# Splitting the weights of a two-layer decoder with casting and adding DMA transfers from GpSimd instead of a VectorE subtraction

## The chip, the cores and the metric

The kernel runs on one core of one Trainium2 chip. The metric is the device time of one execution in microseconds; before the change three runs gave a median of 1575.38 us (1574.05 to 1576.89).

A core has five engines with their own instruction streams: PE (TensorE, matrix products; PEld is its weight loads), ACT (ScalarE), DVE (VectorE), POOL (GpSimd) and SP (SyncE, which only issues transfers here). Sixteen DMA engines move data between memory (HBM) and the on-chip SBUF. Each engine works its stream in order and waits on semaphores where it needs another's result.

## The reference

A decoder trunk on 512 tokens of width 1024, with two layers. Each layer is a mixer, a cross-attention into 256 memory tokens, and a gated MLP, all on normalised inputs and added to the running x.

```python
for l in range(DEPTH):                       # DEPTH = 2
    h = rmsnorm(x, norm_mix[l])
    if l % 2 == 0:                           # conv branch + differential attention
        x = x + even_mixer(h, even_w_in[e], ..., even_w_out[e], lam_init)
    else:                                    # stick-breaking attention, 16 heads
        x = x + odd_mixer(h, odd_w_qkv[o], odd_w_out[o])
    x = x + mem_attention(rmsnorm(x, norm_xattn[l]), rmsnorm(mem, norm_mem[l]),
                          x_w_q[l], x_w_kv[l], x_q_gain[l], x_k_gain[l], x_w_out[l])
    x = x + conv_ffn(rmsnorm(x, norm_ffn[l]), ffn_w_up[l], ffn_conv[l], ffn_w_down[l])
return x

def conv_ffn(h, w_up, w_conv, w_down):       # w_up 1024 x 5632, w_down 2816 x 1024
    u = causal_dwconv(h @ w_up, w_conv)
    gate, val = jnp.split(u, 2, axis=-1)
    return (jax.nn.silu(gate) * val) @ w_down
```

All inputs and outputs are float32. What matters for the change are the products `h @ w`: every weight matrix is used once per execution, against all 512 tokens (or all 256 memory tokens for `x_w_kv`).

## The kernel before

**Two parts per operand.** Every float32 operand is carried as hi + lo, both of the type float32r: hi is the value rounded to float32r, lo is what is left. A product of two such operands takes three matmuls, hi x hi, hi x lo and lo x hi (`lin_stream`). For activations and for weights alike, ACT writes hi (a cast) and DVE writes lo = source - hi (`split`, and for weights `prep`).

**The weight stream.** `weight_groups` lists all weights in the order of use, as groups of four column chunks of 128 (or eight, or two) by up to eight chunks of 128 rows. They lie in memory as 260 slots of 128 x 1024 float32 (512 KB), most groups being four slots. `loads` (L571) issues one SP transfer per slot into a `raw` buffer; `prep` (L589) casts it into a `hi` buffer on ACT (L388) and subtracts it into a `lo` buffer on DVE (L403), then frees the raw buffer. The pools hold 3 raw, 5 hi and 5 lo buffers, handed out in turn. The first group (`V`) is loaded in halves of 256 KB, between the chunks of x.

**The matmuls.** `lin` starts one `lin_stream` for each column chunk (or token block) of a group; each accumulates over all row chunks into one of three PSUM accumulators (`acc`) and then spawns the work that takes the result out. In a gated-MLP group of four slots A, B, C, D each slot holds two row chunks of four columns, so a column takes six matmuls of each slot, and the group 96 matmuls of 512 columns. A slot's hi and lo buffers are free when its last column has used them. All four slots are read by every column, so the buffers come free only while the last column runs. The groups of the memory's keys and values (`KV`) have only two token blocks and take 48 matmuls for four slots.

**What sets the order.** The program is written as streams that yield operations. `Issue` keeps a modelled clock per engine, gives each operation a modelled duration, and puts the operations in one static order per engine: of those that can start first, the one with the smallest priority number. An allocation (`AL`) waits until a pool has a free buffer. So the order of a queue such as SP's or POOL's is fixed when the program is built, and at run time each instruction waits, in that order, for the semaphores of what it needs. POOL's stream holds the adds of the norms' squares (`nacc`), small powers for the norms (`s`, `k`), masks and clears (L452, L457); it issues no transfer.

**Names in the profile.** `acc<-hs,hi` and `acc<-hs,lo` are matmuls of activation chunks with weight parts, `acc<-h,...`, `acc<-hi,hs` and the like the same with other activation tiles or the operands exchanged. `raw<-wts` is a weight load, `hi<-raw` ACT's cast, `lo<-raw,hi` DVE's subtraction. L439 is `mm`, L448 `dma`.

Of the kernel before, what the change touches and what calls it, by code (L numbers as in the profile page):

```python
# [14 lines left out]
ALU = mybir.AluOpType  # L15
# [16 lines left out]
def weight_groups():  # L32
    """(name, source, layer, k-chunks, column starts of the 128-wide column chunks)"""
# [95 lines left out]
class T:  # L129
    """a tile and the times of its last accesses"""  # L130
# [55 lines left out]
class Op:  # L186
    __slots__ = ("eng", "dur", "reads", "writes", "fn")

    def __init__(self, eng, dur, reads, writes, fn):
        self.eng, self.dur, self.fn = eng, dur, fn  # L190
        self.reads = [x for x in reads if isinstance(x, V)]
        self.writes = [x for x in writes if isinstance(x, V)]
# [17 lines left out]
class Issue:  # L210
# [24 lines left out]
    def issue(self, op, start):  # L235
        ins = None
        prev = self.last.get(op.eng)
        if prev is None:
            ins = op.fn()
        else:  # L240
            with self.tc.issue_after(prev):
                ins = op.fn()
        self.last[op.eng] = ins.ins
        if op.eng == "SP":
            self.free_at["SP"] = start + 0.5
            b = max(start + 1.2, self.dma_at)
            self.dma_at = b + op.dur
            end = self.dma_at + 1.0
        else:
            end = start + op.dur  # L250
            self.free_at[op.eng] = end
        self.issued(op, start, end, ins.ins)
        for x in op.reads:
            assert x.t.known, "an operation reads a tile that none before it writes"
            for p in x.parts():
                x.t.r[p] = max(x.t.r[p], end + LAT[op.eng])
        for x in op.writes:
            x.t.known = True
            for p in x.parts():
                x.t.w[p] = (end, op.eng)  # L260
# [80 lines left out]
def trunk(ctx: ExitStack, tc: tile.TileContext, xT: bass.AP, memT: bass.AP, wts: bass.AP, par: bass.AP, outT: bass.AP):  # L341
# [11 lines left out]
    pRAW = pool("raw", 3)  # L353
    pHI = pool("hi", 5)
# [94 lines left out]

    def memset(out, val):  # L450
        out = vw(out)
        return Op("POOL", 0.05 + out.n() * 0.0007, [], [out], lambda: nc.gpsimd.memset(out.ap, val))  # L452
# [15 lines left out]
    def stack_q(qs, ps):  # L468
        """qs[s]: rows of part s: hi; the other 64 rows: lo (s = 0, 1: rows 0-63, 64-127 of ps)"""
        for s, (a, b) in enumerate(HALVES):  # L470
            yield act(qs[s][a], ps[a])
            yield tt(qs[s][b], ps[a], qs[s][a].f32(), ALU.subtract)

    def stack_k(kd, kl, ps, scale=None):
        """kd[s]: part s of ps, hi, in both halves of the rows; kl: lo"""
        for s, (a, b) in enumerate(HALVES):
            sc = 1.0 if scale is None else scale[a]
            yield act(kd[s][a], ps[a], scale=sc)
            if scale is None:
# [43 lines left out]
    def warm():  # L523
        """keeps the tensor engine busy until the first operands are there, for its clock"""
# [6 lines left out]
    def setup2():  # L531
# [16 lines left out]
        # dist[p, c] = p + 384 - c: query row p of the block whose slice ends at column 512  # L548
# [18 lines left out]
    raws, prepped = {}, {}  # L567
# [3 lines left out]
    def loads():  # L571
        for gi in range(len(GROUPS)):
            for d in extra.get(gi, ()):
                yield from d()
            for s in range(NSLOT[gi]):
# [9 lines left out]
                else:  # L585
                    yield dma(raw.v(), src, SLOT)
                raws[gi, s] = raw

    def prep():  # L589
        for gi in range(len(GROUPS)):  # L590
            for s in range(NSLOT[gi]):
                hi, lo = yield [AL(pHI, F32R, (P, SLOT), parts=2), AL(pLO, F32R, (P, SLOT), parts=2)]
                if gi == 0:
                    for j in range(2):
                        js = slice(j * 512, j * 512 + 512)
                        yield Until(lambda: (gi, s, j) in raws)
                        raw = raws[gi, s, j]
                        yield act(hi[:, js].p(j), raw[:, js].p(j))
                        yield tt(lo[:, js].p(j), raw[:, js].p(j), hi[:, js].p(j).f32(), ALU.subtract)
                        prepped[gi, s, j] = (hi, lo)  # L600
                else:
                    yield Until(lambda: (gi, s) in raws)
                    raw = raws[gi, s]
                    yield act(hi, raw)
                    yield tt(lo, raw, hi.v().f32(), ALU.subtract)
                    prepped[gi, s, 0] = prepped[gi, s, 1] = (hi, lo)
                free(raw)
# [49 lines left out]
    def lin_done(*names):  # L657
        """all matmuls of these groups have been issued"""
# [19 lines left out]
    def rpow(out, src, n, scale):  # L678
        """out = (src * scale + eps) ** -0.5"""
# [57 lines left out]
    # x chunks: F[name, k] is the tile once its last update has been issued  # L737
# [10 lines left out]
    # ================= layer 0 mixer =================  # L748
# [10 lines left out]
    def qk_even(name, N):  # L759
        # [s][128, head, token]  # L760
# [50 lines left out]
    def put_pt(th, tl, src, i, done=None):  # L811
        """transpose the (i+1) key chunks of query block i and store them at key chunk c, query block i"""
# [99 lines left out]
    def conv3(src, wname, base, step, t):  # L912
        """causal width-3 depthwise convolution along the tokens"""
# [37 lines left out]
    class Lazy(dict):  # L951
        """activation chunks that appear as they are produced"""
# [64 lines left out]
    def head_norm(ps, rc):  # L1017
        """[128 tokens, 2 heads x 256]: normalised, and its transpose [features, (head, dc, token)]"""
# [175 lines left out]
    # ================= gated MLP =================  # L1194
# [83 lines left out]
        # 1 where the key is not strictly before the query (same slicing as dist)  # L1278
# [32 lines left out]
    def stick_head(pr, j):  # L1311
# [10 lines left out]
        for c in range(NB):  # L1322
# [4 lines left out]
            # rows 0-63: hi parts' product and hi x lo; rows 64-127: lo x hi  # L1327
# [23 lines left out]
    def stick(xin, xout):  # L1351
# [4 lines left out]
        def proj(a):  # L1356
# [18 lines left out]
            # [128 keys, key chunk, head, hi | lo, 64]  # L1375
# [103 lines left out]
    spawn(loads(), 3.0)  # L1479
    spawn(prep(), 3.0)  # L1480
# [44 lines left out]
```

## Time and profile before

| | |
|---|---|
| three runs, median (lowest to highest) | 1575.38 us (1574.05 to 1576.89) |
| profiled execution, span from first to last instruction | 1574.8 us |
| PE busy in it | 1550.8 us |
| DVE, ACT, POOL busy | 1048.2, 750.0, 175.7 us |
| granted TensorE clock, mean | 0.997 |
| read from memory in all | 142.92 MB |

The profile gives the span of the profiled execution and no other time of it; the median of the runs is 0.6 us longer. How to read it: the busy share of an engine is an average over stages. The chain of work that ended last is followed back from the end and names, for each stretch of time, the engine and line that set it; idle time of an engine off that chain costs nothing. In the groups of instructions a row reads: line, engine, operation, out<-in, shapes, count | busy us, mean ns of one | idle time of the engine before them and what ended it. In the views of stretches (windows) a row holds the stretch, its length, each engine's busy time with its count of instructions, the granted clock, the share of the 16 DMA engines that is busy, and GB/s.

### The profile page before, as it was taken

How to read it: one execution, taken by the hardware profiler on the slowest of the kernel's cores; microseconds unless marked ns; L12 is line 12 of the kernel's file. 1: busy time of each engine (PE TensorE's matmuls, PEld its weight loads, DVE VectorE, ACT ScalarE, POOL GpSimd, SP SyncE). 2: the span in 40 equal slices, each digit the busy share in tenths (PEclk: the TensorE clock that was granted, in tenths of full speed). 3: DMA queues.
4: the chain of work that ended last, by engine and by line, in shares of the span. 5: the costliest groups of instructions: out<-in, count | busy, mean ns of one | idle time of the engine just before them, and what ended most of it. 6: DMA issues, size and time to landing. Idle time of an engine off the chain costs nothing.

```text
span 1574.8 us, 19182 instructions
## 1 busy us (share of the span) xinstructions
PE 1550.8 (98%) x7242; PEld 1264.2 (80%) x7242; DVE 1048.2 (67%) x1594; ACT 750.0 (48%) x1298; POOL 175.7 (11%) x218
## 2 busy tenths in 40 slices
PE   8999999999999999999999999999999999999999
PEld 6776788788788888888888778787887888888887
DVE  6687756565777457555688887876566765477443
ACT  6566445553534234323577777664544443244221
POOL 4211220200200000000321121202002000000000
PEclk9999999999999999999999999999999999999999
DMA  6212436321233332233221112252113223332232
GB/s 205 70 54 67 127 104 194 110 68 54 64 97 107 107 96 83 89 107 107 81 81 54 48 61 81 80 175 94 54 54 106 88 76 106 107 107 93 76 99 80
DMA packets 42428, 146.26 MB, mean 93 GB/s; under 512 B 4832, under 2 KB 4832, under 8 KB 42336
## 3 DMA queue, kind: packets, MB, share of 16 engines
q1 hardware_dynamic: 42336, 145.04, 29.5%
q8 instruction: 57, 0.93, 0.2%
q14 instruction: 35, 0.29, 0.1%
HBM read 142.92 MB, written 2.10 MB: 92 GB/s over the span
## 4 chain that ended last, share of the span: by engine, by line
PE 88%; DVE 6%; POOL 2%; issue 2%; ACT 2%; DMA 0%; SPq 0%; POOLq 0%; DVEq 0%; ACTq 0%
PE acc L439 77%; PE sc L439 5%; PE pv L439 3%; PE tr L443 3%; POOL nacc L403 2%; DVE hs L409 1%; DVE lo L403 1%; DVE x L403 1%; DMA x<-xT 0%; PE tr L439 0%; ACT hs L391 0%; DVE g L1300 0%; DVE g L403 0%; ACT hi L388 0%; DVE h L403 0%
## 5 line engine op out<-in xcount | busy, mean ns | idle before, releaser
L439 PE MATMUL acc<-hs,hi 128*128 128x512 f32 x1952 | 615.4, 394 | 0.2
L439 PEld LDWEIGHTS acc<-hs,hi 128*128 128x128 f32 x1952 | 365.6, 189 | 78.9 <-issue 3.2
L388 ACT CAST hi<-raw 128x1024 fp32r<-128x1024 f32 (+1 forms) x264 | 271.9, 1035 | 244.4 <-PE acc L439 171.7
L439 PE MATMUL acc<-hs,lo 128*128 128x512 f32 x976 | 383.4, 393 | 4.4 <-DVE lo L403 4.3
L403 DVE TENSOR_TENSOR lo<-raw,hi 128x1024 fp32r<-128x1024 f32 (+1 forms) x264 | 321.9, 1231 | 60.9 <-ACT hi L388 57.9
L439 PE MATMUL acc<-hi,hs 128*128 128x512 f32 (+1 forms) x960 | 280.8, 370 | 0.9 <-ACT hs L391 0.7
L439 PEld LDWEIGHTS acc<-hs,lo 128*128 128x128 f32 x976 | 184.0, 189 | 44.2 <-DVE lo L403 5.7
L439 PE MATMUL acc<-h,hi 128*128 128x512 f32 x704 | 216.2, 389 | 0.0
L439 PEld LDWEIGHTS acc<-hi,hs 128*128 128x128 f32 x960 | 173.1, 190 | 33.6 <-issue 3.1
L439 PE MATMUL acc<-lo,hs 128*128 128x512 f32 (+1 forms) x480 | 176.0, 368 | 5.6 <-DVE lo L403 5.6
L409 DVE SCALAR_TENSOR_TENSOR g<-c,pp,g 128x511 f32<-128x511 f32 (+1 forms) x176 | 132.1, 750 | 56.7 <-ACT g L391 53.6
L403 DVE TENSOR_TENSOR x<-x,acc 128x512 f32<-128x512 f32 x104 | 70.8, 683 | 145.0 <-PE acc L439 144.9
L439 PEld LDWEIGHTS acc<-h,hi 128*128 128x128 f32 x704 | 132.1, 188 | 27.5
L391 ACT ACTIVATE g<-c,pp 128x512 f32<-128x512 f32 x88 | 63.7, 723 | 154.4 <-DVE c L403 154.4
L439 PE MATMUL acc<-h,lo 128*128 128x512 f32 x352 | 136.4, 389 | 0.0
L403 POOL TENSOR_TENSOR nacc<-nacc,sq 128x512 f32<-128x512 f32 x36 | 56.8, 1578 | 524.5 <-ACT sq L391 475.0
L403 DVE TENSOR_TENSOR c<-acc,rrow 128x512 f32<-128x512 f32 x92 | 63.5, 691 | 70.8 <-PE acc L439 63.9
L439 PEld LDWEIGHTS acc<-lo,hs 128*128 128x128 f32 x480 | 90.8, 189 | 22.0 <-DVE lo L403 7.3
L439 PE MATMUL acc<-y,hi 128*128 128x512 f32 x256 | 81.5, 394 | 0.6 <-ACT y L388 0.6
L439 PEld LDWEIGHTS acc<-h,lo 128*128 128x128 f32 x352 | 66.1, 188 | 13.7
L403 DVE TENSOR_TENSOR g<-g,g 128x512 f32<-128x512 f32 (+2 forms) x112 | 64.7, 578 | 7.8 <-ACT g L388 1.4
L391 ACT ACTIVATE g<-sc,rq 128x128 f32<-128x128 f32 (+3 forms) x128 | 60.9, 530 | 8.8 <-PE sc L439 6.5
(157 smaller groups left out, 1624.7 us busy)
## 6 DMA issues: line engine op xcount, KB each, us to landing
raw<-wts SPq DMA_DIRECT2D x256, 512.0 KB, 4.1
x<-xT SPq DMA_DIRECT2D x16, 256.0 KB, 4.8
raw<-wts SPq DMA_DIRECT2D x8, 256.0 KB, 5.9
raw<-memT SPq DMA_DIRECT2D x4, 512.0 KB, 4.2
outT<-x SPq DMA_DIRECT2D x8, 256.0 KB, 2.0
pp<-par SPq DMA_DIRECT2D x1, 303.5 KB, 5.4
pp<-par SPq DMA_DIRECT2D x1, 4.0 KB, 1.7
```

The lines of the kernel that those rows point to most:

```text
L388: return nc.scalar.copy(out=out.ap, in_=in_.ap)
L391: return nc.scalar.activation(out=out.ap, in_=in_.ap, func=func, scale=_raw(scale), **kw)
L403: lambda: _ve(eng).tensor_tensor(out=out.ap, in0=in0.ap, in1=in1.ap, op=op))
L409: lambda: nc.vector.scalar_tensor_tensor(out=out.ap, in0=in0.ap, scalar=_raw(scalar), in1=in1.ap, op0=op0, op1=op1))
L439: lambda: nc.tensor.matmul(out.ap, lhsT.ap, rhs.ap, start=start, stop=stop))
L443: return Op("PE", 0.109, [in_, ident_v], [out], lambda: nc.tensor.transpose(out.ap, in_.ap, ident_v.ap))
```

## The change

From the second group on, a slot is no longer loaded raw by SP, cast by ACT and subtracted by DVE. Instead POOL issues a casting transfer from memory into the hi buffer (`prep_hi`), ACT writes lo = -hi, and POOL issues a second transfer of the same weights that adds them to the lo buffer (`accum_op=ALU.add`), which makes lo = w - hi. The raw pool goes from 3 to 2 buffers, the hi pool from 5 to 6. The first group keeps the old path. `Op` and `Issue` get a modelled duration for POOL's transfers (1.1 us of POOL's time in the model); removed comments and blank lines are left out here.

```diff
-    __slots__ = ("eng", "dur", "reads", "writes", "fn")
+    __slots__ = ("eng", "dur", "reads", "writes", "fn", "land")
...
+        elif op.land is not None:
+            self.free_at[op.eng] = start + op.dur
+            b = max(start + op.dur + 1.0, self.dma_at)
+            self.dma_at = b + op.land
             end = self.dma_at + 1.0
...
-    pRAW = pool("raw", 3)
-    pHI = pool("hi", 5)
+    pRAW = pool("raw", 2)
+    pHI = pool("hi", 6)
     pLO = pool("lo", 5)
...
+    def pool_dma(out, in_, n, **kw):
+
+        out = vw(out)
+        return Op("POOL", 1.1, [out] if kw else [], [out], lambda: nc.gpsimd.dma_start(out=out.ap, in_=in_, **kw),
+                  land=n * P * 4 / 358.0e3)
...
-            for s in range(NSLOT[gi]):
+            for s in range(NSLOT[gi] if gi == 0 else 0):
...
-                else:
-                    yield dma(raw.v(), src, SLOT)
                 raws[gi, s] = raw
+
+    def prep_hi():
+
+        for gi in range(1, len(GROUPS)):
+            for s in range(NSLOT[gi]):
+                if gi == 1 and s == 0:
+                    yield Until(lambda: (0, NSLOT[0] - 1) in raws)
+                hi = yield AL(pHI, F32R, (P, SLOT), parts=2)
+                yield pool_dma(hi, wts[FIRST[gi] + s], SLOT)
+                his[gi, s] = hi
 
     def prep():
         for gi in range(len(GROUPS)):
             for s in range(NSLOT[gi]):
+                if gi:
+                    yield Until(lambda: (gi, s) in his)
+                    hi = his[gi, s]
+                    lo = yield AL(pLO, F32R, (P, SLOT), parts=2)
+                    yield act(lo, hi.v().f32(), scale=-1.0)
+                    yield pool_dma(lo, wts[FIRST[gi] + s], SLOT, accum_op=ALU.add)
+                    prepped[gi, s, 0] = prepped[gi, s, 1] = (hi, lo)
+                    continue
...
-                else:
-                    yield Until(lambda: (gi, s) in raws)
-                    raw = raws[gi, s]
-                    yield act(hi, raw)
-                    yield tt(lo, raw, hi.v().f32(), ALU.subtract)
-                    prepped[gi, s, 0] = prepped[gi, s, 1] = (hi, lo)
                 free(raw)
...
     spawn(loads(), 3.0)
+    spawn(prep_hi(), 2.95)
     spawn(prep(), 3.0)
```

How the instructions are placed, at two points inside the first gated MLP.

The weight transfers for one group. Before, they stand on SP, one per slot, each waiting for the DVE subtraction that frees a raw buffer:

```order
L448 DMA raw_4678<-wts 128x1024 [waits DMAHW1_49,DVE_49]
L448 DMA raw_4690<-wts 128x1024 [waits DMAHW2_49,DVE_49]
L448 DMA raw_4702<-wts 128x1024 [waits DMAHW3_49,DVE_49]
L448 DMA raw_4724<-wts 128x1024 [waits DMAHW4_49,DVE_49]
L448 DMA raw_4806<-wts 128x1024 [waits DMAHW5_49,DVE_49]
```

Now they stand on POOL, eight per group. With A, B, C, D for a group's slots, the first two rows are hi of C and D, the next two hi of A and B of the following group, then lo of B, C, D and of the following A. A hi row waits for PE (the buffer of six allocations earlier), a lo row for ACT's lo = -hi; DMASW are the semaphores of POOL's earlier transfers:

```order
L458 DMA hi_4842<-wts 128x1024 [waits DMASW3_49,PE_49]
L458 DMA hi_4855<-wts 128x1024 [waits DMASW4_49,PE_49]
L458 DMA hi_4864<-wts 128x1024 [waits DMASW5_49,PE_49]
L458 DMA hi_4874<-wts 128x1024 [waits DMASW6_49,PE_49]
L458 DMA lo_4843<-wts 128x1024 [waits DMASW7_49,Activation_49]
L458 DMA lo_4887<-wts 128x1024 [waits DMASW0_49,Activation_49]
L458 DMA lo_4899<-wts 128x1024 [waits DMASW1_49,Activation_49]
L458 DMA lo_4910<-wts 128x1024 [waits DMASW2_49,Activation_49]
```

SP issued the loads of a group as raw buffers came free; POOL now issues all four hi transfers ahead of the first lo transfer, and both kinds stand in one queue.

The matmuls of the same stage on PE. Before, a column (one accumulator) goes through all four slots in one piece; hi_4827, hi_4940 are the group's slots A and B:

```order
L439 MATMUL acc_4899<-hs_3655,hi_4827 128x512
L439 MATMUL acc_4899<-hs_3656,hi_4827 128x512
L439 MATMUL acc_4899<-hs_3655,lo_4828 128x512
L439 MATMUL acc_4899<-hs_3657,hi_4827 128x512
L439 MATMUL acc_4899<-hs_3658,hi_4827 128x512
L439 MATMUL acc_4899<-hs_3657,lo_4828 128x512
L439 MATMUL acc_4899<-hs_3659,hi_4940 128x512
L439 MATMUL acc_4899<-hs_3660,hi_4940 128x512
L439 MATMUL acc_4899<-hs_3659,lo_4941 128x512
```

Now three columns (acc_4809, acc_4838, acc_4880) first take slot A and two hi products of slot B, eight matmuls each, and only then does the first column go on with lo_4843 (B), hi_4842 and lo_4887 (C), hi_4855 and lo_4899 (D). These are the 23rd to the 34th matmul of the group:

```order
L444 MATMUL acc_4880<-hs_3594,hi_4727 128x512
L444 MATMUL acc_4880<-hs_3595,hi_4727 128x512
L444 MATMUL acc_4809<-hs_3594,lo_4843 128x512
L444 MATMUL acc_4809<-hs_3596,hi_4727 128x512
L444 MATMUL acc_4809<-hs_3597,hi_4727 128x512
L444 MATMUL acc_4809<-hs_3596,lo_4843 128x512
L444 MATMUL acc_4809<-hs_3598,hi_4842 128x512
L444 MATMUL acc_4809<-hs_3599,hi_4842 128x512
L444 MATMUL acc_4838<-hs_3594,lo_4843 128x512
L444 MATMUL acc_4809<-hs_3598,lo_4887 128x512
L444 MATMUL acc_4809<-hs_3641,hi_4842 128x512
L444 MATMUL acc_4809<-hs_3642,hi_4842 128x512
```

The first use of the lo tiles of B, C and D has moved behind the start of three columns: lo of B is read first by the 25th matmul of the group, lo of C by the 32nd, lo of D by the 39th. The last column still takes the four slots one after the other, six matmuls each.

More of the change, by code (lines that the diff above doesn't have):

```diff
@@ L186, with __init__ @@
 class Op:
-    __slots__ = ("eng", "dur", "reads", "writes", "fn")
-    def __init__(self, eng, dur, reads, writes, fn):
-        self.eng, self.dur, self.fn = eng, dur, fn
+    __slots__ = ("eng", "dur", "reads", "writes", "fn", "land")
+    def __init__(self, eng, dur, reads, writes, fn, land=None):
+        self.eng, self.dur, self.fn, self.land = eng, dur, fn, land
         self.reads = [x for x in reads if isinstance(x, V)]
@@ L247, in issue @@
             self.dma_at = b + op.dur
+            end = self.dma_at + 1.0
+        elif op.land is not None:
+            self.free_at[op.eng] = start + op.dur
+            b = max(start + op.dur + 1.0, self.dma_at)
+            self.dma_at = b + op.land
             end = self.dma_at + 1.0
@@ L564, in setup2 @@
         F["bias"] = bias
-    raws, prepped = {}, {}
+    raws, prepped, his = {}, {}, {}
     extra = {}
@@ L591, in prep @@
             for s in range(NSLOT[gi]):
-                hi, lo = yield [AL(pHI, F32R, (P, SLOT), parts=2), AL(pLO, F32R, (P, SLOT), parts=2)]
[L593 to L600, printed above, removed]
-                else:
-                    yield Until(lambda: (gi, s) in raws)
-                    raw = raws[gi, s]
-                    yield act(hi, raw)
-                    yield tt(lo, raw, hi.v().f32(), ALU.subtract)
-                    prepped[gi, s, 0] = prepped[gi, s, 1] = (hi, lo)
+                if gi:
[6 more added lines that the diff above has]
+                    continue
+                hi, lo = yield [AL(pHI, F32R, (P, SLOT), parts=2), AL(pLO, F32R, (P, SLOT), parts=2)]
+                for j in range(2):
+                    js = slice(j * 512, j * 512 + 512)
+                    yield Until(lambda: (gi, s, j) in raws)
+                    raw = raws[gi, s, j]
+                    yield act(hi[:, js].p(j), raw[:, js].p(j))
+                    yield tt(lo[:, js].p(j), raw[:, js].p(j), hi[:, js].p(j).f32(), ALU.subtract)
+                    prepped[gi, s, j] = (hi, lo)
                 free(raw)
```

## The prediction

> **What bounds the kernel now.** First the busy times, then the chain that ended last in order of time, then what PE waited for.
>
> ```profile
> span 1574.8 us, 19182 instructions
> PE 1550.8 (98%) x7242; PEld 1264.2 (80%) x7242; DVE 1048.2 (67%) x1594; ACT 750.0 (48%) x1298; POOL 175.7 (11%) x218
> PE 88%; DVE 6%; POOL 2%; issue 2%; ACT 2%; DMA 0%; SPq 0%; POOLq 0%; DVEq 0%; ACTq 0%
> 416.44 340.08 PE acc L439 x1500
> 1218.79 352.30 PE acc L439 x1554
> PE acc L439 <- DVE lo L403: 9.8, 6, 2.1
> ```
>
> PE is idle for only 1574.8 - 1550.8 = 24.0 us. The two long rows of the chain are the two gated MLPs: 692 us in which one weight matmul follows the other and nothing else counts, 340.08 / 1500 = 0.2267 us each. The subtraction that the change takes from DVE holds PE up for 9.8 us in the whole run. So the change has at most 24 us to win, about 10 of it directly, and everything hangs on whether the weights still come in time.
>
> ```profile
> L388 ACT CAST hi<-raw 128x1024 fp32r<-128x1024 f32 (+1 forms) x264 | 271.9, 1035 | 244.4 <-PE acc L439 171.7 <-DMA raw<-wts 70.4
> L403 DVE TENSOR_TENSOR lo<-raw,hi 128x1024 fp32r<-128x1024 f32 (+1 forms) x264 | 321.9, 1231 | 60.9 <-ACT hi L388 57.9
> 525.00:750.00 225.00, 48.33 (x40) 42.47 (x41) 1.00 0.30 96
> raw<-wts SPq DMA_DIRECT2D x256, 512.0 KB, 4.1
> ```
>
> Before, the load of a slot (512 KB) is done long ahead, into a raw buffer. From the moment in which PE gives a hi and a lo buffer back, only ACT (1.04 us) and DVE (1.23 us) stand before the next use. The third row (window, its length, DVE and ACT on raw tiles, clock, DMA share, GB/s) prices a load: in 225 us at 96 GB/s 21.6 MB moved, 41.2 slots, in 0.30 x 225 = 67.5 us of all 16 engines, so **1.64 us of DMA time per slot**. From issue to landing it takes 4.1 us, so 4.1 - 1.64 = 2.46 us are latency.
>
> **What is removed.** 256 loads on SP's queue and 256 subtractions on DVE (some 315 us of its 1048). They lie beside PE; I count -10 us for the waits quoted above, and 0 to -24 as bounds. ACT keeps one pass per slot over as many elements, now lo = -hi: nothing, since the same engine is as busy as before.
>
> **What is added.** 256 casting loads and 256 adding transfers on POOL's queue. The second reads the weights again and adds them to what is in SBUF. Take a group of the MLPs: four slots A, B, C, D, 96 matmuls, 21.8 us at 0.2267. By the order, POOL issues for each group four casting loads (slots C and D of this group, A and B of the next), then four adding transfers (B, C, D, and A of the next), in this sequence. The first of the eight, hi of C, needs the hi buffer of six allocations earlier: that of A in the group before, which PE gives back 18 matmuls before that group's end (the fourth column's last three slots, 6 each). The seventh, lo of D, is read first by the 39th matmul of the group. Between the two lie 18 + 38 = 56 matmuls, **12.70 us**. In this window go one issue, the latency and seven transfers, four casting and three adding, on the same 16 engines.
>
> Terms whose price the trace doesn't show, with the nearest rows:
>
> ```profile
> L448 SPq DMA_DIRECT2D raw<-wts x264: 327/328/527, 1.2 to 1538.4; - x132
> L403 POOL TENSOR_TENSOR s<-s,mhalf 128x2 f32<-128x2 f32 (+2 forms) x36 | 35.3, 981 | 219.3 <-DVE s L419 206.9 <-DVE s L424 8.4 <-DVE k L403 4.0
> L403 POOL TENSOR_TENSOR nacc<-nacc,sq 128x512 f32<-128x512 f32 x36 | 56.8, 1578 | 524.5 <-ACT sq L391 475.0 <-issue 47.6
> outT<-x SPq DMA_DIRECT2D x8, 256.0 KB, 2.0
> ```
>
> - A DMA issue on POOL: between SP's 0.33 us and POOL's own 1.58 us instruction. I take 1.0, since POOL needs 981 ns even for 128x2 elements.
> - A casting load: between the plain 1.64 us and 1.64 + 1.04 (ACT's cast of the same tile laid on top) = 2.68. I take 1.64: it moves the same bytes, once in and once out.
> - An adding transfer: at least the plain 1.64 us. It must take in a second stream of 512 KB, the tile in SBUF; SBUF is not free to read for a DMA (the stores, 256 KB, take 2.0 us to land). I take two streams through the same engines, 3.28 us. Upper end: POOL's adder on the tile (2 x 1.58) on top of a load, 4.80.
> - A gain in any of the three is excluded by the bytes: none moves fewer than the plain load.
>
> So the window needs 1.0 + 2.46 + 4 x 1.64 + 3 x 3.28 = 19.86 us and has 12.70: **PE stands 7.16 us in each MLP group**. The MLPs hold 132 of the 260 slots, 33 groups: +236 us. With plain 1.64 for the adding transfers it is 14.94, so +2.24 per group, +74; with 2.68 and 4.80 it is 28.58, +15.9, +524.
>
> The eight memory key/value groups (32 slots) have two blocks of tokens only, 48 matmuls or 10.9 us for four slots. Four casts and four adds take 4 x (1.64 + 3.28) = 19.7 us of the engines: +8.8 each, +70 in all (plain 13.1: +18; upper 29.9: +152).
>
> ```profile
> 208.04 37.11 PE acc L439 x163
> 193.00:280.00 87.00, 86.30 (x391) 70.78 (x391) 54.14 (x69) 44.00 (x71) 12.28 (x11) 1.00 0.48 151
> ```
>
> These rows are such a stretch today: PE back to back with the DMA engines at 0.48 of their time.
>
> The other 23 groups (the first group keeps the old path) share the rest, 1574.8 - 692 - 87 = 796 us, so 34.6 us each where the MLP has 21.8; the difference is attention and norms. If the window grew in proportion it would be 20.2 us, just the 19.86 needed; but attention comes in lumps and some groups have none. I take half of the MLP's stall, 3.58 x 23 = +82; ends 0 and the full 165.
>
> A smaller edit: raw buffers 3 to 2 matter for the first group alone, and the norm's adds and powers on POOL now stand behind DMA issues that wait for PE.
>
> ```profile
> 1199.66 1.79 POOL nacc L403
> 1207.99 1.60 POOL nacc L403
> 1209.60 6.52 issue
> ```
>
> Such a norm is already on the chain (here POOL adds from 1199.66 to 1209.6). A DMA issue or two among its rows costs 1 to 3 us in each of 8 norms: 0 to 24, inside the other terms' ends, and I take 0.
>
> Sum against the profiled execution: 1574.8 + 236 + 70 + 82 - 10 = **1953 us**. The median of the runs, 1575.38, is 0.6 above that span; I say 1950.
>
> **Two rules of the Trainium skill.** The row says 4.1 us from issue to landing for 512 KB. The Trainium skill, "DMA: Bandwidth & Descriptors", section "Anatomy of one DMA", fits a GpSimd-issued transfer by 2.0 us plus bytes over 436 GB/s. By that a plain slot moves in 1.2 us; an estimate for the window with doubled adds is then 1.0 + 2.0 + 4 x 1.2 + 3 x 2.4 = 15.0 us, +2.3 per group and some 1670 us in all, and with plain adds 11.4, no stall. The trace's own load is slower (1.64 us where the page's fit has 1.2), so I stay with the row. The second speaks against the change too:
>
> ```profile
> L419 DVE TENSOR_SCALAR c<-c,s 128x256 f32<-128x256 f32 x32 | 9.9, 351 | 0.6
> L419 DVE TENSOR_SCALAR s<-s 128x2 f32<-128x2 f32 (+2 forms) x52 | 9.5, 183 | 22.8 <-ACT sq L391 22.2
> L419 DVE TENSOR_SCALAR s<-s,k 128x2 f32<-128x2 f32 (+1 forms) x32 | 7.3, 227 | 19.3 <-POOL s L403 19.2
> ```
>
> "SBUF — State Buffer", section "Who interferes with whom", has the Trainium skill say that a DVE copy or tensor_scalar in a two-port mode locks GpSimd out while it writes descriptors. The rows of that kind sum to 26.7 us, so by the rule 1953 becomes at most 1980; without it 1953. No run here shows it.
>
> **The rivals.**
> - *The adding transfer costs a plain one.* Sum: 1574.8 + 74 + 18 + 26 (half of 2.24 x 23) - 10 = 1683. For it: the load's floor may be the memory's, which the SBUF side doesn't share. Against: two streams must enter where one did.
> - *Adding or casting is slower than streaming.* With 2.68 and 4.80: 1574.8 + 524 + 152 + 183 - 10 = 2424, and 2607 with the other groups' full 366. For it: every adder in the profile (DVE 1.23 us, POOL 3.16 us per slot) takes as long as the load or longer. Against: nothing in the trace.
> - *Not slower:* the seven transfers fit. The place is the same window, 12.70 us; it decides at (12.70 - 1.0 - 2.46) / 7 = 1.32 us per transfer, adds included. Then PE never waits and DVE's waits are gone: 1551 to 1575 us. Against: no stretch of the trace moves a slot in that.
>
> ```profile
> DMA  6212436321233332233221112252113223332232
> GB/s 205 70 54 67 127 104 194 110 68 54 64 97 107 107 96 83 89 107 107 81 81 54 48 61 81 80 175 94 54 54 106 88 76 106 107 107 93 76 99 80
> ```
>
> The best slice moves 205 GB/s at 6 tenths busy, so 293 to 342 GB/s at full; 524 KB in 1.32 us would be 397.
>
> **How the numbers follow.** Two streams, 1800 to 2100 us: 0.40. Plain price, 1640 to 1800: 0.18. Slower adding or casting, 2100 to 2600: 0.26; beyond 2600, an adder worse than any row: 0.09. Fits: 0.07, of it 0.05 faster by over 0.2% and 0.02 within 0.2%, which is about what a measurement of this kernel tells from no change. Slower: 0.93. The range's low end is the plain price with nothing lost in the 23 other groups and all of PE's idle time won, 1574.8 + 74 + 18 - 24 = 1643; its high end the slow price in full, 2607. It leaves 0.16 out.
>
> **What would show it.** In the profile of the changed kernel: PE waits in the MLPs named by lo tiles and a DMA, some 7 us per group of 96 matmuls; the MLP windows at DMA shares near 0.7 (19.7 of 29 us); the POOL queue's issues near 1 us; the landing of an adding transfer several us above that of a casting one; DVE down by some 315 us without effect. Wrong if PE keeps its 0.2267 us rows through the MLPs, if the wait falls on hi tiles (then casting is the dear one), or if the engines stay idle while PE waits (then latency or the queue's order, and not the second stream, sets the time).

## The result, and the profile after

The changed kernel takes 1907.6 us (median of 4 runs, 1901.3 to 1917.9) against 1575.7 us (4 runs beside them): **1.211 times as long, 95% interval 1.206 to 1.215**. The prediction was 1950 us and slower. The first view is the page of the changed kernel; the lines are in the order of the ones shown for the kernel before.

```profile
span 1899.2 us, 19269 instructions
PE 1658.3 (87%) x7242; PEld 1305.1 (69%) x7242; DVE 759.6 (40%) x1338; ACT 745.7 (39%) x1298; POOL 526.2 (28%) x730
...
q0 software_dynamic: 73728, 268.47, 60.4%
...
issue 48%; PE 22%; POOL 16%; DMA 10%; DVE 3%; ACT 2%; POOLq 0%; SPq 0%; DVEq 0%; ACTq 0%
...
hi<-wts POOLq DMA_DIRECT2D x256, 512.0 KB, 5.3
lo<-wts POOLq DMA_DIRECT2D x256, 512.0 KB, 8.8
```

The chain was 88% PE; now it is POOL's issues, DMA and "issue", with 22% PE. DVE lost 288.6 us of work (1048.2 before), and the total shows no gain from it. PE is idle for 240.9 us where it was idle for 24.0, and its 7242 matmuls are busy for 107.5 us more (1658.3 against 1550.8), while the mean granted clock fell from 0.997 to 0.951. What PE waited for (engine, line, releaser: us in total, times, longest) has one row that counts:

```profile
PE acc L444 <- DMA lo<-wts: 208.3, 95, 8.5
```

Inside one MLP group, POOL's timeline (start, length, what, idle time before it and what ended it) and three stretches (length, busy time of PE, PEld, DVE, ACT and POOL, clock, DMA share, GB/s):

```profile
584.12 0.56 POOL L458 DMA_DIRECT2D hi<-wts  x1 [17.41 <-PE acc L444]
585.48 0.55 POOL L458 DMA_DIRECT2D hi<-wts  x1 [0.80 <-PE acc L444]
586.84 0.53 POOL L458 DMA_DIRECT2D hi<-wts  x1 [0.81 <-PE acc L444]
588.20 0.53 POOL L458 DMA_DIRECT2D hi<-wts  x1 [0.83 <-PE acc L444]
588.72 0.93 POOL L458 DMA_DIRECT2D lo<-wts  x1
...
593.91 0.86 POOL L458 DMA_DIRECT2D lo<-wts  x1 [0.86 <-ACT lo L396]
```

```profile
584.00:594.00 10.00, 9.56 (x43) 7.58 (x41) 4.61 (x7) 5.96 (x8) 4.92 (x8) 1.00 0.78 222
594.00:603.00 9.00, 6.19 (x19) 4.71 (x20) 0.69 (x1) 0.13 (x1) 0.77 (x1) 0.81 1.06 211
604.00:612.00 8.00, 8.00 (x37) 6.64 (x36) 6.31 (x9) 3.83 (x6) 0.56 (x1) 1.00 0.00 0
```

Read them together. POOL sits for 17.41 us until PE gives the first buffer back, then issues all eight transfers within 10 us. The DMA engines are full while PE stands (second stretch), and do nothing at all in the third, while PE runs at its full rate. The engines have time enough over the group; they are not allowed to use it. Over 200 us of MLP their share is 0.65:

```profile
600.00:800.00 200.00, 177.06 (x717) 139.78 (x716) 64.52 (x91) 54.60 (x68) 39.80 (x56) 0.94 0.65 151
```

A second table is worked out from the matmul records of each trace: the time from the last matmul of one group of weights to the last of the next, summed by stage. "Inner group" is the median over the 28 MLP groups of four slots that do not follow a norm. The first group is counted from the start of the trace, some 10 us ahead of the first instruction, so the three stages of a row add up to more than the span; between rows this makes less than 1 us.

| kernel | time, us | inner MLP group | both MLPs | 8 key/value groups | the rest |
|---|---|---|---|---|---|
| before | 1575.7 | 21.76 | 730.7 | 91.8 | 759.2 |
| after | 1907.6 | 27.21 | 914.7 | 131.2 | 859.5 |
| e1_no_second | 1569.7 | 21.76 | 725.4 | 92.4 | 753.0 |
| e2_plain_second | 1755.7 | 24.23 | 824.1 | 110.6 | 825.6 |
| e3_lo_first | 1804.0 | 25.52 | 858.4 | 129.0 | 822.0 |
| e4_buffers | 1751.6 | 24.58 | 828.5 | 123.3 | 802.7 |
| e5_both | 1741.6 | 24.69 | 813.3 | 121.8 | 808.7 |
| e6_cast_only | 1615.1 | 21.76 | 737.3 | 109.3 | 778.6 |
| e7_add_only | 1890.8 | 26.66 | 894.8 | 145.6 | 852.9 |
| e8_fill | 1906.5 | 27.16 | 913.1 | 131.0 | 873.3 |
| e9_after_norms | 1620.4 | 21.76 | 742.5 | 91.9 | 783.6 |
| e10_pairs | 1782.4 | 23.13 | 793.6 | 130.1 | 863.2 |
| e11_pairs_both | 1671.1 | 21.76 | 741.9 | 122.9 | 802.9 |
| e12_norm_dve | 1596.1 | 21.76 | 733.6 | 91.7 | 780.0 |

The first column holds the medians of the runs, the others one profiled execution each. The change costs +184.0 us in the MLPs, +39.4 in the key/value groups and +100.3 in the rest.

### The profile page after: what moved, and what is told of

It is laid out like the page before. It is cut to its first block, busy times and chain, and to the rows that moved or that the text cites. A ratio compares the mean times of both kernels' runs of the same rounds, so it can differ in the third digit from the quotient of the medians.

```text
span 1899.2 us, 19269 instructions
## 1 busy us (share of the span) xinstructions
PE 1658.3 (87%) x7242; PEld 1305.1 (69%) x7242; DVE 759.6 (40%) x1338; ACT 745.7 (39%) x1298; POOL 526.2 (28%) x730
## 4 chain that ended last, share of the span: by engine, by line
issue 48%; PE 22%; POOL 16%; DMA 10%; DVE 3%; ACT 2%; POOLq 0%; SPq 0%; DVEq 0%; ACTq 0%
PE acc L444 16%; DMA lo<-wts 9%; POOL lo L458 7%; POOL hi L458 6%; PE sc L444 3%; POOL nacc L408 2%; PE tr L448 1%; PE pv L444 1%; DVE hs L414 1%; POOL s L408 1%; DMA hi<-wts 0%; ACT hs L396 0%; ACT sq L396 0%; DVE g L1320 0%; PE tr L444 0%
## 5 line engine op out<-in xcount | busy, mean ns | idle before, releaser
L444 PE MATMUL acc<-hs,hi 128*128 128x512 f32 x1952 | 631.7, 406 | 1.3 <-DVE x L408 1.3
L444 PE MATMUL acc<-hs,lo 128*128 128x512 f32 x976 | 401.0, 418 | 92.4 <-DMA lo<-wts 92.0
L444 PEld LDWEIGHTS acc<-hs,hi 128*128 128x128 f32 x1952 | 381.2, 196 | 82.8 <-issue 2.4
L396 ACT ACTIVATE lo<-hi 128x1024 fp32r<-128x1024 f32 x256 | 268.8, 1055 | 367.7 <-PE acc L444 246.6
L458 POOL DMA_DIRECT2D hi<-wts x256 | 142.8, 560 | 832.6 <-PE acc L444 825.6
L444 PEld LDWEIGHTS acc<-hs,lo 128*128 128x128 f32 x976 | 193.1, 198 | 161.1 <-DMA lo<-wts 120.0
L458 POOL DMA_DIRECT2D lo<-wts x256 | 228.5, 907 | 173.8 <-ACT lo L396 160.8
L444 PE MATMUL acc<-lo,hs 128*128 128x512 f32 (+1 forms) x480 | 185.2, 388 | 59.3 <-DMA lo<-wts 58.3
L444 PE MATMUL acc<-h,hi 128*128 128x512 f32 x704 | 224.7, 406 | 0.0
L444 PE MATMUL acc<-y,lo 128*128 128x512 f32 x128 | 53.9, 421 | 19.7 <-DMA lo<-wts 19.7
```

The source lines that it names most:

```text
L396: return nc.scalar.activation(out=out.ap, in_=in_.ap, func=func, scale=_raw(scale), **kw)
L444: lambda: nc.tensor.matmul(out.ap, lhsT.ap, rhs.ap, start=start, stop=stop))
L458: return Op("POOL", 1.1, [out] if kw else [], [out], lambda: nc.gpsimd.dma_start(out=out.ap, in_=in_, **kw), land=n * P * 4 / 358.0e3)
```

## The experiments

**Theory 1** is the prediction's: in a window between the release of a slot's buffers and the first use of the lo parts, so many transfers must pass through full engines. The rivals differ by run.

**e1_no_second**: the adding transfer alone is taken away.

```diff
-                    yield pool_dma(lo, wts[FIRST[gi] + s], SLOT, accum_op=ALU.add)
```

> The second transfer is left out (lo stays -hi), so the kernel does everything of the change but the 256 adding transfers. Theory 1 (PE waits for a burst of transfers on the DMA engines: four casts at about 1.6 us and three adds at about 2.6 us between the release of a group's first slot and the first use of the next group's lo tiles): the four casts alone fit, MLP groups of 96 matmuls back at 21.8 us, 1560 to 1590 us in all. Rival (the casting load itself is what comes late, landing in 5.3 us where the plain load took 4.1, and now issued only when a buffer is free): PE still waits, on hi tiles, and the time stays above 1650 us.

Measured: 1569.7 us, ratio 0.995 (0.994 to 0.997), span 1564.5, inside theory 1's range. The casting transfers are hidden; PE is at its full rate in the MLPs. POOL's queue on the page, the landing, and one stretch of MLP price them:

```profile
q0 software_dynamic: 36864, 134.23, 27.8%
...
hi<-wts POOLq DMA_DIRECT2D x256, 512.0 KB, 4.7
```

```profile
600.00:800.00 200.00, 199.96 (x925) 166.16 (x923) 82.17 (x118) 84.39 (x117) 31.70 (x49) 1.00 0.31 96
```

256 casts took 0.278 x 1564.5 = 434.9 us of all 16 engines, 1.70 us each; the stretch gives 62 us for 36.6 slots, 1.69. In the changed kernel the same queue holds 0.604 x 1899.2 = 1147.1 us, so an adding transfer takes (1147.1 - 434.9) / 256 = **2.78 us**, if a cast costs the same beside adds. These are prices by busy share; what transfers take back to back stands with the prediction below.

**e2_plain_second**: the same order, buffers and waits, but the second transfer overwrites lo instead of adding to it.

```diff
-                    yield pool_dma(lo, wts[FIRST[gi] + s], SLOT, accum_op=ALU.add)
+                    yield pool_dma(lo, wts[FIRST[gi] + s], SLOT)
```

> The second transfer overwrites lo instead of adding to it (lo = w, the -hi pass of ScalarE stays): same order of every instruction, same bytes from memory, only the read and add in SBUF are gone. Theory 1: the transfer falls from 2.6 to about 1.6 us, the wait for slot B's lo from 3.2 to about 2.2 us, an MLP group from 27.2 to 24 us or less, the memory key/value groups from 16 to 13 us; 1720 to 1800 us in all. Rival (order and latency: the first lo transfer stands behind four hi issues and takes 7 us to land whatever it does): unchanged within 2%, 1870 to 1930 us.

Measured: 1755.7 us, ratio 1.113 (1.108 to 1.118). That is inside theory 1's range. 152 us of the loss are the adding; 180 us are left with a second transfer that adds nothing but stands in the same place. Its landing falls from 8.8 to 6.1 us:

```profile
hi<-wts POOLq DMA_DIRECT2D x256, 512.0 KB, 5.0
lo<-wts POOLq DMA_DIRECT2D x256, 512.0 KB, 6.1
```

**e3_lo_first** and **e4_buffers**: the order of the two kinds on POOL, and the raw buffers' place given to hi and lo.

```diff
-    spawn(prep_hi(), 2.95)
+    spawn(prep_hi(), 3.05)
```

> prep_hi gets priority 3.05 instead of 2.95, so that a lo transfer that is ready goes ahead of a hi transfer: in an MLP group the first lo stands second in POOL's queue instead of fifth. Same transfers, same bytes. Theory 1: the burst is as long, but the first lo lands some 4 us earlier and only the last one is late, 3.5 + 3 x 1.6 + 3 x 2.6 = 16.1 us against the window of 12.7, so about 3.4 us per group instead of 5.4: some 1820 us. Rival (order): the waits go almost wholly, below 1700 us.

```diff
-    pRAW = pool("raw", 2)
-    pHI = pool("hi", 6)
-    pLO = pool("lo", 5)
+    pHI = pool("hi", 7)
+    pLO = pool("lo", 6)
+    pRAW = pHI
```

> The two raw buffers are given to the others (raw tiles are taken from the hi pool; hi 7, lo 6 buffers), nothing else. Theory 1: two slots instead of one are complete when a group starts, so the first late tile is lo of slot C, for which five transfers (four casts, one add) must pass: 3.5 + 6.4 + 2.6 = 12.5 us against 54 matmuls, 12.2 us; MLP groups near 23 us, 1650 to 1750 us in all. Rival (the engines are too slow for two transfers per slot at any depth): MLP groups stay above 26 us, since 4 x (1.6 + 2.6) = 16.8 us of engine time per group would have to be the limit, and the time above 1850 us.

Measured: 1804.0 us (ratio 1.143, 1.138 to 1.149) and 1751.6 us (1.110, 1.105 to 1.115). Neither removes a byte, and they win 104 and 156 us. So the engines' total is not what binds. The first is near the 1820 us of theory 1. The second lies 2 us above its range, with groups of 24.58 us where some 23 were expected: the expectation counted 54 matmuls up to the lo part of slot C, but the trace has it read by the 32nd matmul, 18 + 31 = 49 after the release.

**e5_both**: the two edits together.

> The two edits of e3_lo_first and e4_buffers together: the adding transfers go ahead of the casting ones in the planner, and the raw buffers' place gives one hi and one lo buffer more (7 hi, 6 lo). Theory 1 (a window between the release of a buffer and the first use of its lo part, in which so many transfers must pass; the engines have time enough over a whole MLP group, 4 x (1.70 + 2.78) = 17.9 of 21.8 us): order and window each gave about 100 and 155 us, and together they must give more than either; MLP groups below 24 us, total 1640 to 1730. Rival (the casting and adding transfers simply slow each other on the engines, or lose a fixed time per group whatever the order): no better than the better of the two, 1740 to 1810. In neither case below 1575: the key/value groups need 17.9 us for 10.9.

Measured: 1741.6 us, ratio 1.105 (1.101 to 1.108): a miss for theory 1, which wanted MLP groups below 24 us and got 24.69. The two edits do not add, and the number is the rival's. PE's timeline there shows two short stops per group, each for a lo part:

```profile
669.16 0.50 PE L444 MATMUL acc<-hs,lo 128*128 128x512 f32 x1 [1.06 <-DMA lo<-wts]
676.47 0.50 PE L444 MATMUL acc<-hs,lo 128*128 128x512 f32 x1 [1.55 <-DMA lo<-wts]
```

Two readings were left: the engines lose time whenever casts and adds overlap, or the burst still starts too late, since all four releases lie in the last column. e10 and e11 tell them apart.

**e6_cast_only** and **e7_add_only**: the kernel before with one half of the change each (`pool_dma` and its modelled duration come with it, the pools stay).

```diff
...
+                    yield pool_dma(hi, wts[FIRST[gi] + s], SLOT)
                     yield Until(lambda: (gi, s) in raws)
                     raw = raws[gi, s]
-                    yield act(hi, raw)
                     yield tt(lo, raw, hi.v().f32(), ALU.subtract)
```

> The kernel before with one part of the change: hi by a casting transfer from GpSimd in place of ACT's cast; the raw slot is still loaded by SP and lo is still DVE's subtraction. So each slot is moved twice, and nothing is added in memory. Theory 1: in the window of the MLPs stand 1.0 + 2.46 + 3 x 1.70 + 1.23 = 9.8 us against some 12.7, no stall; key/value groups 4 x (1.70 + 1.64) = 13.4 for 10.9 us, +20 in all: 1570 to 1610. Rival (it is the doubled traffic of the weights, or transfers issued from GpSimd behind PE's releases, that costs most of the 180 us left in e2_plain_second, which also moves each slot twice): 1650 to 1760.

```diff
...
                     yield act(hi, raw)
-                    yield tt(lo, raw, hi.v().f32(), ALU.subtract)
+                    yield act(lo, hi.v().f32(), scale=-1.0)
+                    yield pool_dma(lo, wts[FIRST[gi] + s], SLOT, accum_op=ALU.add)
```

> The kernel before with the other part: raw by SP and hi by ACT's cast as before, lo = -hi by ACT, and the adding transfer from GpSimd in place of DVE's subtraction. Two transfers per slot, one of them adding. Theory 1: to the last lo of an MLP group 2 x 1.04 + 0.9 + 2.46 + 3 x 2.8 = 13.8 us against 12.7, +1.1 for 33 groups, and the loads far ahead compete with the adds for the engines; key/value groups 4 x (1.64 + 2.8) = 17.8 for 10.9 us, +55; 1640 to 1730. Rival (the adding transfer is dear in itself, wherever the casts are, by its latency of 8.8 us from issue to landing): 1800 to 1910.

Measured: 1615.1 us (ratio 1.025, 1.020 to 1.029) and 1890.8 us (1.199, 1.195 to 1.203). The first lies 5 us above the range; the MLP groups stay at 21.76 and the key/value groups take +17.5, as expected, but the rest takes +19. So loading each slot twice is not dear by itself. The second is a clear miss, and its number is the rival's. Three stretches of one of its MLP groups say why:

```profile
601.00:609.00 8.00, 8.00 (x37) 6.64 (x36) 7.00 (x10) 4.99 (x7) 0.00 (x0) 1.00 0.00 1
613.00:626.00 13.00, 10.03 (x37) 7.47 (x36) 2.88 (x4) 3.90 (x5) 1.76 (x3) 0.87 1.04 259
627.00:635.00 8.00, 8.00 (x37) 6.61 (x36) 1.95 (x3) 1.05 (x1) 0.00 (x0) 1.00 0.01 1
```

My expectation had put the raw loads "far ahead". They are not: a raw buffer comes free when ACT reads it, ACT reads it when PE releases hi, and so the four loads of the next slots start in the same moment as the four adds. Eight transfers stand in the same burst; the engines are full for these 13 us and idle in the two stretches of 8 us. It is the changed kernel's pattern with loads in the casts' place. At least 2.9 us of the latency that the rival names are this queueing: with only 20 slots on the new path an adding transfer lands after 6.3 us (the page of e9_after_norms), not after the 9.2 of e7_add_only.

```profile
lo<-wts POOLq DMA_DIRECT2D x20, 512.0 KB, 6.3
```

**e8_fill**: 1 us of small transposes on PE, ahead of the wait in each MLP group.

```diff
+                if s == 1 and GROUPS[gi][0][0] in "UD" and gi not in filled:
+                    filled.add(gi)
+                    w = yield AL(aPV)
+                    for i in range(8):
+                        yield tp(w[:, i % 4 * P:(i % 4 + 1) * P], ident_t)
+                    free(w)
                 yield mm(ps, wl, ah, False, z)
...
```

> The changed kernel with eight small transposes into an unused accumulator on PE, some 1.3 us, put once into each of the 33 MLP groups ahead of the first use of the second slot's lo part. PE's stop there is then some 2 us instead of 3.25. Theory 1 (the transfers set the time; the half clock that follows a stop of over 3 us is only what PE does while it would wait for the lo parts of the third and fourth slot anyway): the granted clock rises to about 0.99, new waits stand at the later lo parts, and the time stays within 1880 to 1920. Rival (the half clock is a cost of its own, 3.41 us at half speed, 1.7 us in each of 33 groups): 1840 to 1865.

Measured: 1906.5 us (ratio 1.210, 1.205 to 1.214). The time is the one theory 1 gave, but not the clock, which stayed at 0.949: the stop went from 3.25 to 2.32 us (medians of the 28 inner groups), and the half clock still followed it in most groups. New waits did come at the later lo parts: in 17 of the 28 groups PE stands there for 0.3 us or more, in 4 of 28 without the transposes. As the clock did not rise, the run alone does not tell the two apart; the landing times do, at the end of the part on the prediction.

**e10_pairs** and **e11_pairs_both**: the columns of an MLP group run in pairs, slot by slot; in e11 on top of e5_both.

```diff
+            if kind == "f" and GROUPS[gi][0][0] in "UD":
+                yield Until(lambda: pos_of.get((gi, m ^ 1), 0) >= s)
             yield Until(lambda: (gi, s, j) in prepped and ki in A)
...
+            if ki % 2 or ki == nk - 1:
+                pos_of[gi, m] = s + 1
...
```

> The changed kernel with another order of PE's matmuls in the MLPs alone: the four columns of a group run as two pairs, each pair slot by slot, where before column after column ran through all four slots. The first slot's buffers then come free 36 matmuls before the group's end and not 18; the same transfers, buffers and arithmetic. Theory 1 (eight transfers, 17.9 us of full engines, are bunched behind the release of the buffers, and what counts is the time from the first release to the first use): the window is 18 x 0.2267 = 4.1 us longer, the MLP groups go from 27.2 us to 23 to 24, the total to 1730 to 1800. Rival (the stall is a fixed latency of each adding transfer, or the engines' total): groups stay above 26 us, 1870 to 1920.

> The order of e10_pairs with the two edits of e5_both (adding transfers first, 7 hi and 6 lo buffers). Theory 1: the engines need 17.9 us per MLP group of 21.8, and the window is now longer than the e5_both groups lacked (2.8 us): MLP groups at 21.8 to 22.3, granted clock near 1.0, total 1742 - 33 x 2.6 = 1656, so 1635 to 1680; what is left over 1575 stands in the key/value groups and around the norms. Rival (casting and adding slow each other whenever they overlap, so that the 24.6 us of e5_both are the engines' own): 1720 to 1745.

Measured: 1782.4 us (ratio 1.130, 1.128 to 1.133) and 1671.1 us (1.059, 1.055 to 1.063), both inside theory 1's ranges. The same 200 us of MLP in e11_pairs_both:

```profile
600.00:800.00 200.00, 199.88 (x883) 165.15 (x882) 77.25 (x110) 70.38 (x86) 53.94 (x77) 1.00 0.84 194
```

PE is busy for 199.88 of 200 us with both streams of every weight in flight, engines at 0.84. This settles e5: casts and adds may overlap, and the loss in the MLPs was the window. It is also the answer to e7's rival, since every add is still there, landing after 7.6 us.

**e9_after_norms** and **e12_norm_dve**: the kernel before with the changed path for 20 of 260 slots, the five groups that follow a norm (lines that choose the path are left out below); in e12 the norm's adds go from POOL to DVE.

```diff
+    NEW = [GN[n] for n in ("Q0_0", "U0_0", "SQK0", "Q0_1", "U0_1")]
...
-            yield tt(N["acc"], N["acc"], sq, ALU.add, eng="POOL" if k < KD - 1 else "DVE")
+            yield tt(N["acc"], N["acc"], sq, ALU.add, eng="POOL" if N["x"] == "x0" else "DVE")
```

(the last two lines in e12_norm_dve only)

> The kernel before, with the changed path for five groups of weights only: those that follow a norm on the path (queries of both cross-attentions, first group of both MLPs, first query/key group of the second mixer), 20 of 260 slots; pools as before. From e1_no_second: with DVE free of the weights these places took 10 us less (2.2 to 2.7 us each at the queries and the first MLP groups). Theory 1: there PE stands still for a norm, so 3.46 us, three casts and an add (11.4 us to the second lo part) are mostly hidden by it, and the next group is on the old path, so nothing accumulates: 1563 to 1574. Rival (the adding transfers are late even there, as in the changed kernel, where the first MLP group takes 36 us for 28): 1580 to 1610.

> The kernel of e9_after_norms (changed path only for the five groups after a norm) with one edit: the adds of the norms' squares, six of about 1.6 us each on POOL, go to DVE. In e9_after_norms the casting transfers of these groups stood behind those adds in POOL's queue, 6 us or more after their buffers were free, and the first MLP group took 33.7 us against 28.1 before. Theory (at the norms the cost of the change is POOL's queue): the casts are issued when PE releases the buffers, the last lo part lands after 18.6 us, in a window that the norm's own stop widens to about 19; first MLP groups at 25 to 28.5 us, total 1560 to 1585. Rival (the window is too short there in any case): first MLP groups above 31 us, total 1600 to 1620.

Measured: 1620.4 us (ratio 1.028, 1.026 to 1.030), above both ranges, and 1596.1 us (1.012, 1.010 to 1.014). POOL's timeline at the first MLP of e9:

```profile
410.94 9.93 POOL L408 TENSOR_TENSOR nacc<-nacc,sq 128x512 f32<-128x512 f32 x6 [8.60 <-ACT sq L396]
420.81 1.65 POOL L458 DMA_DIRECT2D hi<-wts  x3
```

The casting transfers stand behind six adds of the norm, and no wait is shown ahead of them: their buffers had been free for some 6 us (in e12 PE releases them at 414.43). With the adds on DVE the two first MLP groups take 28.9 and 30.2 us where they took 33.7 and 34.2 (28.1 before), and the kernel 24 us less. The groups lie just above the 25 to 28.5 us expected, and the time missed e12's range by 11 us: the query groups stay at 35.8 and 32.9 us against 27.0 and 28.5 before, for a reason that no run here isolates. Moving the adds also changes the norm itself, and the kernel before was not run with that edit alone. No version here that does the whole work is faster than the kernel before.

## Why the prediction was right, and where it was off

- **What binds, and where: right.** The stall stands at lo parts and the DMA, in the MLPs first, with POOL's issues released by PE. e10 and e11 show the window as the cause. The wait was named at the fourth slot's lo part. In the trace PE stands at the second slot's and then goes on at half clock, but the fourth's still sets the pace: by the landing times it lands 17.6 us after the group's first issue (median of the 28 inner groups), and PE reads it within 0.04 us of its landing in 15 of them, within 0.4 us in 27.
- **The casting transfer, 1.64 us: right** as a mean price (1.70). **DVE's waits, -10: right** (e1: 1569.7 against 1576.6 beside it, -7 us).
- **The adding transfer, 3.28 us: too dear, but not by its factor of two.** It takes 2.78 us by its queue's share, 1.64 of a casting one. Back to back, though, the adds of a burst land 2.49 us apart in the changed kernel, and the same transfers without the adding 1.27 us apart in e2 (medians of 170 pairs each): a factor of 2.0. What was too dear is the price that was doubled: 1.64 us was read off loads that were spread out, and a busy share is no rate. A stretch of e2 without the adding (share and GB/s are the last two figures), against 1.06 and 211 in the second stretch of the changed kernel above:

```profile
604.00:607.00 3.00, 1.52 (x7) 1.19 (x7) 0.00 (x0) 0.00 (x0) 0.53 (x1) 1.00 1.12 414
```

- **An issue, 1.0 us: too dear.** The first of a group is a cast, 0.56 (an add 0.9). With the shares' prices the prediction's own sum for the window is 0.56 + 2.46 + 4 x 1.70 + 3 x 2.78 = 18.16, less 12.70: 5.46 us per group, where 27.21 - 21.76 = 5.45 were measured. That the two agree to 0.01 us is luck: the trace has 17.6 us, and the sum leaves out that PE gives the hi buffers back one by one. For e4 it gives +2.68 (two adds in the window: 15.38; measured +2.82). For e2 it gives +2.22 (seven plain transfers: 14.92; measured +2.47), but there the second slot's lo part binds, with stops of 2.03 us, and the fourth's lands 0.8 us before its use. So the MLP term was +184 and not +236 mainly because of the adding transfer's size.
- **Key/value groups, +70: too large** (+39.4). These are bound by the engines, as said:

```profile
1200.00:1275.00 75.00, 59.47 (x236) 43.34 (x234) 13.03 (x27) 30.25 (x48) 29.98 (x42) 0.95 1.03 259
```

  At 259 GB/s a slot's two passages of 524 KB take 4.05 us, so four slots 16.2, and a group took 131.2 / 8 = 16.4. The prediction had 19.7, from the same 3.28, and started from 10.9 where the eight groups average 91.8 / 8 = 11.5. By the shares' prices it would be 4 x (1.70 + 2.78) = 17.9, by the back-to-back ones 4 x (1.27 + 2.49) = 15.0.
- **The other 23 groups, +82: right in size** (+100.3), by a guess, and its miss of +18 hides part of the -52 and -31 of the other two terms. Groups of weights alone (EO, SO1) lose 6 us like the MLPs, most attention groups 1 to 4.
- **What would show it: right** on the named waits, on adds landing later than casts (8.8 against 5.3 us), on DVE's 289 us without effect, and nearly on the MLPs' DMA share (0.65 for 0.7); the 7 us per group were 5.45.
- **The norms, 0: wrong, and the wrong way round.** The prediction had the norm's adds stand behind transfers. What happens is that transfers stand behind the norm's adds. In the changed kernel, first POOL, then PE:

```profile
462.86 9.93 POOL L408 TENSOR_TENSOR nacc<-nacc,sq 128x512 f32<-128x512 f32 x6 [17.00 <-ACT sq L396]
472.74 1.16 POOL L458 DMA_DIRECT2D hi<-wts  x2
```

```profile
486.26 0.80 PE L444 MATMUL acc<-hs,lo 128*128 128x512 f32 x1 [5.88 <-DMA lo<-wts]
```

  The two first MLP groups lost 8.0 and 7.6 us, of which an inner group loses 5.45 too. These belong to the +184; in e11, where inner groups lose nothing, the two still take 33.4 us each (28.1 before), and in e9 all five groups behind a norm cost 36 us together.
- **Two rules of the Trainium skill.** "DMA: Bandwidth & Descriptors", section "Anatomy of one DMA", has 2.0 us plus bytes over 436 GB/s for a GpSimd-issued transfer: by estimate 3.2 us for a slot. In e1, where casts are alone on POOL's queue, the median landing is 4.7 us and the shortest 3.7, so the trace does not agree with that time; with the rate it nearly does, as e2 moves 414 GB/s when its transfers follow each other. The 1670 us by that rule were too low, and with the 23 other groups counted as in the main sum they would have been some 1695. "SBUF — State Buffer", section "Who interferes with whom", would have a VectorE copy or tensor_scalar in a two-port mode hold up GpSimd's writing of descriptors. The issues on POOL (count: shortest/median/longest ns) leave little room for it in the changed kernel:

```profile
L458 POOL DMA_DIRECT2D hi<-wts x256: 530/546/909, 14.2 to 1856.8; - x128
L458 POOL DMA_DIRECT2D lo<-wts x256: 853/881/1582, 23.3 to 1877.1; - x128
```

  The sums of the two, 142.8 and 228.5 us, lie 6 us above 256 medians of each.

**The half clock** (below) is hardly a cost of its own in the inner groups. With every lo part landing when it did and every matmul at 0.2267 us, the inner groups would be 0.16 us shorter in the median, and 7 us in all 28 together: PE would stand at the later lo parts instead. This is an estimate from the landing and matmul records of the changed kernel, with the landings held fixed. What the half clock costs outside these groups stays open.

## What to carry to other kernels

When work moves from a compute engine into transfers that write the final buffer, ask when that buffer comes free, not how busy the DMA engines are on average: here they stood idle for a third of each group and still set the time, because eight transfers could start only when PE let go. The remedy was an order of the consumer that releases buffers evenly (all of the MLPs' inner loss came back with it, the larger pools and the adds ahead of the casts), and not fewer bytes. Take a transfer's price from transfers that follow each other, not from a busy share. And look at every instruction that the issuing engine's queue already holds: behind 10 us of a norm's adds the casts of e9 left some 6 us after their buffers were free.

## What the runs showed of the hardware that was not expected

- An adding transfer into SBUF moves its 512 KB at 211 GB/s when adds alone are in flight (594 to 603 us above), where a mix of plain loads and adds moves 259 (e7_add_only) and the same transfers without the adding move 414 (e2, 604 to 607 us). The adding halves the rate, at a busy share above 1 in all three. In the queues' shares over the whole run it costs only 1.64 times a casting one.
- After a stop of PE the granted clock was often half for some 3.4 us, but not by the length of the stop alone. In e7_add_only, two neighbouring groups, PE's timeline and a stretch soon after each stop:

```profile
617.30 0.50 PE L444 MATMUL acc<-h,lo 128*128 128x512 f32 x1 [2.65 <-DMA lo<-wts]
...
644.23 0.50 PE L444 MATMUL acc<-h,lo 128*128 128x512 f32 x1 [2.86 <-DMA lo<-wts]
```

```profile
619.00:620.00 1.00, 1.00 (x4) 0.81 (x3) 0.00 (x0) 0.00 (x0) 0.00 (x0) 0.50 1.01 279
646.00:647.00 1.00, 1.00 (x6) 0.83 (x5) 0.00 (x0) 0.00 (x0) 0.00 (x0) 1.00 1.06 274
```

  The shorter stop was followed by half clock, the longer was not.
